# A hybrid decoder layer on one core: decay factors made a group sooner, a boundary weight rounded a step later, and the first 128 columns of keys and queries scaled straight from PSUM

## The chip, the cores and the metric

One Trainium2 chip, one core. The kernel is a hand-scheduled Tile program: one instruction stream for each engine, TensorE (PE), VectorE (DVE), ScalarE (ACT), GpSimd (POOL), and SyncE (SP), which issues most DMAs. The metric is device time in microseconds (us) of one launch. The times of the kernel before are 840.01, 841.22 and 841.30 us, with the median 841.22.

## The reference

The layer takes x of 512 tokens by 1024 features in float32 and adds three sub-layers to it, each with a norm ahead and behind:

```python
x = x + 0.5 * rms_norm(swiglu(rms_norm(x, ffn1_pre_g[l]), ffn1_w_gu[l], ffn1_w_down[l]), ffn1_post_g[l])
y = hybrid_mixer(rms_norm(x, mix_pre_g[l]), w_in[l], conv_w[l], conv_b[l], w_rg[l], ...)
x = x + rms_norm(y, mix_post_g[l])
x = x + 0.5 * rms_norm(swiglu(rms_norm(x, ffn2_pre_g[l]), ffn2_w_gu[l], ffn2_w_down[l]), ffn2_post_g[l])
```

`swiglu` has a hidden width of 2816. The mixer projects to four things: the input of a recurrence (512 channels), its gate (512), queries (8 heads of 64), and keys and values (2 heads of 64 each). The recurrence is a causal convolution of width 4, two block-diagonal gate products with a sigmoid, and a linear scan, whose decay is

```python
log_a = LRU_C * r * jax.nn.log_sigmoid(lam.astype(jnp.float32))
a = jnp.exp(log_a)
mult = jnp.sqrt(-jnp.expm1(2.0 * log_a))
```

`lam` has one value for each of the 512 channels, so `LRU_C * log_sigmoid(lam)` needs nothing but a parameter. Attention is banded: each block of 128 queries sees its own block of keys and the one before, and a sink. Block 0 has no block before it.

## The kernel before

Every float32 product is made of three matmuls on rounded parts: a weight is split into a high half (`whi`, cast by ACT) and a low half (`wlo`, what DVE finds by subtracting the high half from the raw weight), activations likewise. The class `Weights` (`W`) keeps three counters: raw weights loaded from HBM into five raw buffers, units rounded, units taken by a product. `W.fill(n)` rounds until `n` units beyond those taken are ready; a raw buffer that is used up is loaded anew at that point. `W.take(ahead)` fills ahead and hands out the next unit. So the place of a `fill` in the program sets where the cast and the subtraction of a weight stand in ACT's and DVE's streams. Each engine runs its stream strictly in the order in which it was written.

The first feed-forward part runs over five groups of hidden chunks (`GROUPS1`: 0-4, 4-8, 8-12, 12-16, 16-22), numbered 0 to 4. Groups 1 to 3 each run `octo`, a gate and an up product of four chunks at once by seven products instead of eight; its seven steps are numbered 0 to 6, each with two weight units and 24 matmuls (line L968), on the tiles `aa`, `da` and `ba`. From group 2 on, `seven_down` (L1362, tiles `yaa`, `yda`, `yba`, `yea`) multiplies the hidden values of the group before by the down weights, and `seven_forms_of` gives `octo` a dictionary `beside` of small steps to run after chosen steps: reading the hidden values back (`hxa`), sums of them (`s1a` to `s4a`) and their high (`hha`, `hhs`) and low (`hla`, `hls`) parts. `yea` is the product with the form `s4`.

`decay_factor` (L1290) computes `ka` = `LRU_C * log_sigmoid(lam)` and `nka` = -`ka` on a tile of 128 by 4: a few DVE operations, one `Exp` on ACT (`z`), and a series on DVE. ACT holds one table of functions at a time. A load of the table with `Exp` comes ahead of `z` (L1301), and a load of the table with `Silu` ahead of the next `Silu` (L995). The two results are first read in the mixer.

After group 4 comes the boundary to the mixer (`boundary`). The last three (`LATE`) of eight output chunks are taken aside as weights, and their products are made in two halves of 256 tokens: first half of chunks 5, 6 and 7, then the second halves. Each half is added to a partial sum (L697, `yp_a`), squared on ACT (L541, `sq_r`), and the squares are gathered (L710 and L714, `accb_r`). From them the statistics are made: a matmul with a mean vector (L555, `rms_r`), a square root on ACT (L561), a reciprocal (L563) and a diagonal tile `dg_r` (L565) on DVE, and a matmul that spreads it over the partitions (L569, `rms_r`). Both matmuls stand inside the second halves of chunks 6 and 7. Behind that the first products of the mixer use the four `xl` weights.

In the mixer, `in_parts` (L1548) takes a key or query product from its PSUM bank, scales it by the norm's factor `R` into a float32 tile, copies its first 128 columns into `home` (L1551), and splits the tile into high and low parts. `home` serves the plain float32 products of block 0 (`cur`, L1661), one call for the keys and four for the queries.

Of the kernel before, what the change touches and what calls it, by code (L numbers as in the profile page):

```python
# [15 lines left out]
P = 128  # L16
# [106 lines left out]
def tile_layer(ctx: ExitStack, tc: tile.TileContext, out: bass.AP, **ins: bass.AP):  # L123
    nc = tc.nc
    pe, dve, act, pool, sync = nc.tensor, nc.vector, nc.scalar, nc.gpsimd, nc.sync
# [37 lines left out]
    def wt(name, w=T, dt=F32):  # L163
        return tmp.tile([P, w], dt, tag="w", name=name, bufs=NW)


    W = Weights()
# [318 lines left out]
    def preload(func):  # L486
        act.activation(dummy, eps, func)
# [5 lines left out]
    def colrange(name):  # L493
        lo, n = col_of[name]
        return cols[:, lo:lo + n]
# [616 lines left out]
    def seven_down(hid, f, one, part, forms, ahead, beside={}, keep=False, hold=False):  # L1112

        free = [r_tile] + 3 * [acc_tile]
        for fn in beside.get(-1, ()):
            fn()
        A, B, Dd, E_ = ([bank(f"y{s}{hid.name}{f}{i}") for i in range(2)] for s in "abde")
        for n, (banks, form, blocks) in enumerate(((A, "a11", []), (Dd, "s3", [(1, 1)]), (B, "a12", [(0, 0)]), (A, "s2", [(1, 0)]),  # L1120
                                    (E_, "s4", [(0, 1)]), (Dd, "a22", [(1, 0)]), (A, "s1", [(1, 1), (0, 1)]))):
            if form == "s3":
                W.fill(AHEAD, True)
                hid.steps.pop(0)()
            one(banks, W.take(ahead if form == "a11" else AHEAD), forms[form], form in ("a11", "s3", "s4"))
            if form == "a11":
                for i in range(2):
                    act.copy(B[i], A[i])
            if hid.steps and form != "s3":
                hid.steps.pop(0)()  # L1130
            for i in range(2 if form in (("s3", "s2") if keep else ("a12", "s3", "s2", "s4") + (() if hold else ("a22", "s1"))) else 0):
                if keep:
                    o = part(*blocks[0], i)
                    dve.tensor_add(o, o, banks[i])
                    continue
                st = (wt if form == "s1" else free.pop() if free else t2k)("stage")
                act.copy(st, banks[i])  # L1137
                for half, dh in blocks:
                    o = part(half, dh, i)
                    pool.dma_start(o, st, accum_op=ALU.add)  # L1140
            for fn in beside.get(n, ()):
                fn()
        return {(0, 0): B, (1, 0): Dd, (0, 1): E_, (1, 1): A}
# [146 lines left out]
    def decay_factor():  # L1290

        lam = colrange("lru_lambda")

        def s4(name):
            return const.tile([P, KC], F32, name=name)

        nabs = s4("nabs")
        dve.tensor_scalar(nabs, lam, -1.0, None, op0=ALU.mult)
        dve.tensor_tensor(nabs, nabs, lam, op=ALU.min)
        z = s4("z")  # L1300
        act.activation(z, nabs, AF.Exp)  # L1301
        s = s4("s")
        dve.tensor_scalar(s, z, 2.0, None, op0=ALU.add)
        dve.reciprocal(s, s)
        dve.tensor_mul(s, s, z)
        s2 = s4("s2")
        dve.tensor_mul(s2, s, s)
        q = s4("q")
        dve.tensor_scalar(q, s2, 1.0 / 15, None, op0=ALU.mult)
        for n in (13, 11, 9, 7, 5, 3):  # L1310
            dve.scalar_tensor_tensor(q, q, 1.0 / n, s2, op0=ALU.add, op1=ALU.mult)
        dve.scalar_tensor_tensor(q, q, 1.0, s, op0=ALU.add, op1=ALU.mult)

        ka = s4("ka")
        dve.tensor_scalar(ka, lam, 0.0, LRU_C, op0=ALU.min, op1=ALU.mult)
        dve.scalar_tensor_tensor(ka, q, -2.0 * LRU_C, ka, op0=ALU.mult, op1=ALU.add)
        nka = s4("nka")
        dve.tensor_scalar(nka, ka, -1.0, None, op0=ALU.mult)
        return ka, nka
# [36 lines left out]
    hid = Hidden("a", n1)  # L1356
# [16 lines left out]
    def read_rows(dh):  # L1373
        if dh:
            t = wpool.tile([P, NB * T], F32, tag="raw", name="rows_a1", bufs=NRAW)
            row_sums[dh] = [t[:, tb * T:(tb + 1) * T] for tb in range(NB)]
        else:
            row_sums[dh] = [r_tile("rows_a00")] + [acc_tile(f"rows_a0{tb}") for tb in range(1, NB)]
        for tb in range(NB):
            sync.dma_start(row_sums[dh][tb], rows_hbm[tb, dh])  # L1380
# [3 lines left out]
    def turn_sums(dh):  # L1384
        z = wpool.tile([P, NB * T], F32, tag="raw", name="zy1", bufs=NRAW) if dh else wide("zy0")
        for tb in range(NB):
            row = row_sums[dh][tb]
            if dh or tb > 1:
                dve.tensor_add(row, row, held[tb // 2, dh][tb % 2])
            dve.transpose(z.rearrange("p (j b n) -> p b j n", n=32, b=NB)[:, tb], row.rearrange("p (j n) -> p j n", n=32))  # L1390
        moves[dh] = z

    def move_sums(dh):
        to = wide(f"yp_a{dh}")
        chunks = to.rearrange("p (c t) -> p c t", c=4)
        turned = moves[dh].rearrange("p (c q n) -> p c q n", c=4, q=4)
        for i in range(4):
            for q in range(4):
                (pool if q % 2 else sync).dma_start(chunks[32 * q:32 * (q + 1), :, i * P:(i + 1) * P], turned[32 * i:32 * (i + 1), :, q])  # L1399
        for c in range(4):  # L1400
            parts[4 * dh + c] = chunks[:, c]
# [26 lines left out]
    def give_back():  # L1428
        tiles, xT[:] = stream()
        for x, h in zip(tiles, xT_hbm):  # L1430
            pool.dma_start(x, h)
        return tiles

    parts = [None] * KD
    late, h_hbm, decay = [], {}, []
    for g, (f0, f1) in enumerate(GROUPS1):
        if g:
            beside = hid.seven_forms_of(before, h_hbm[before], dealt_halves=True) if g > 1 else {}
            if g == 2:
                beside[2] = [lambda: decay.append(decay_factor())]  # L1440
            h_hbm[f0] = hid.octo(f0, beside)
            if g > 1:
                held = seven_down(hid, before, by_dealt_tokens, lambda half, dh, i: rows_hbm[2 * half + i, dh], hid.forms, AHEAD - 1, hold=f1 == FC)
            if f1 == FC:
                held[0, 1] = held[1, 1]
                W.owed = [W.load, W.load, lambda: read_rows(1), lambda: None]
            before = f0
            if f1 < FC:
                continue
            xs = hid.last_chunks(f0, h_hbm[f0], {0: lambda: read_rows(0), 4: lambda: (turn_sums(0), move_sums(0))})  # L1450
            ka, nka = decay[0]
        else:
            hid.in_blocks = True
            first_down(hid.classic(f1, banks, {}))
            hid.in_blocks = False
            continue
        res = Residual("r1", lambda c: half_g[:, c:c + 1])
        turn_sums(1)
        for c in range(KD):
            if c == 0:  # L1460
                load_gates()
            if c == 1:
                move_sums(1)
                preload(AF.Sqrt)
            if c == 3:
                x_tiles[:] = give_back()
            if c >= KD - LATE:
                late.append((c, W.take(0)))
                W.fill(3)
                continue  # L1470
            if c == 0:

                two = [W.take(), W.take()]
                pair_banks = [bank(f"ya{g}{i}") for i in range(2)]
                for k, x in enumerate(xs):
                    for w, b in zip(two, pair_banks):
                        mm3(b, w, k, x, k == 0, k == len(xs) - 1)
            b = pair_banks[c] if c < 2 else product(W.take(), xs, name=f"ya{g}{c}")
            res.chunk(c, b, parts[c])
# [8 lines left out]
    def scaled(t, b):  # L1488
        dve.tensor_mul(t, b, R)
        return t  # L1490
# [53 lines left out]
    R = mx.R  # L1544
# [2 lines left out]

    def in_parts(b, first, name, low=dve):  # L1548

        x = scaled(wt(name), b)  # L1550
        dve.tensor_copy(first, x[:, :P])  # L1551
        if name == "qT3":
            spare.extend(fours("attn", F32R))
            xh, xl = spare.pop(), spare.pop()
        else:
            xh, xl = t2k(f"{name}h", F32R), t2k(f"{name}l", F32R)
        act.copy(xh, x)
        low.tensor_sub(xl, x, xh.bitcast(F32))
        return xh, xl
# [8 lines left out]
    for j in range(4):  # L1568
        b = in_product(f"pq{j}")
# [348 lines left out]
    hid = Hidden("b", n2)  # L1918
# [46 lines left out]
    h_hbm = {}  # L1965
# [27 lines left out]
    for g, (f0, f1) in enumerate(GROUPS2):  # L1993
        if g:
            h_hbm[f0] = hid.octo(f0, hid.seven_forms_of(before, h_hbm[before], (1, 2.5, 3.5, 4.5, 5.5, 6)), f1 == FC)
            kept = seven_down(hid, before, by_tokens, down, hid.forms, AHEAD - 1, *((last, True) if f1 == FC else ()))
            before = f0
# [15 lines left out]
        before = 2  # L2013
# [94 lines left out]
```

## Time and profile before

| what | value |
|---|---|
| median of the runs | 841.22 us (840.01 to 841.30) |
| the profiled execution | 840.68 us |
| its span, first to last instruction | 838.7 us |
| granted TensorE clock, mean | 0.999 |
| TensorE busy | 830.4 us (99%) |
| VectorE busy | 732.4 us (87%) |
| ScalarE busy | 519.2 us (62%) |
| GpSimd busy | 166.8 us (20%) |
| group 2: `octo` and `seven_down` | up to 175.04 us |
| boundary to the mixer | about 330 to 361 us |
| keys and queries of the mixer | about 371 to 408 us |

Rows of a timeline give start, duration, engine, line, operation, names of what is written and read, and in brackets how long the engine had stood idle and what ended that. Matmuls are pipelined: a row's duration is longer than the step to the next row, and a late matmul shows in the steps between starts. A matmul of 512 columns follows the one before by 0.23 us, one of 256 by 0.12. The chain of waits goes back from the last instruction to what released each step; merged rows give start, duration and the line. Rows of stretches give the busy time of each engine, with the number of instructions, the granted clock, the share of the DMA engines and GB/s.

### The profile page before, as it was taken

Reading aid. Unit: us, or ns where it says so; the run is one execution under the profiler, and the core shown is the slowest. Engines: PE = TensorE matmul, PEld = TensorE weight load, DVE = VectorE, ACT = ScalarE, POOL = GpSimd, SP = SyncE. Lnnn points to the kernel's source line nnn. Section 1 sums busy time; section 2 is a strip of 40 time slices with the busy share of each in tenths; the row PEclk is TensorE's granted clock in tenths of the full one; section 3 lists DMA queues with packets and bytes.
Section 4 is the critical chain, followed back from the end, with each engine's and each line's share of the span. In section 5 each row is a group of like instructions: output and inputs, shape, how many; then the busy total and the mean of one; then the engine's idle time right before and its main releaser. Section 6 shows DMA issues by size and latency. Waiting matters only on the chain.

```text
span 838.7 us, 11907 instructions
## 1 busy us (share of the span) xinstructions
PE 830.4 (99%) x4252; PEld 705.9 (84%) x4252; DVE 732.4 (87%) x1036; ACT 519.2 (62%) x813; POOL 166.8 (20%) x188
## 2 busy tenths in 40 slices
PE   9999999999999999999999999999999999999997
PEld 9988888788888898987788899888888888888885
DVE  4989698999989978889789589997999799898996
ACT  6646556586666654556797446545758667676562
POOL 2022000041320325414531052002004023032001
PEclk9999999999999999999999999999999999999999
DMA  7276407299595797522511131667339939769742
GB/s 252 102 274 227 150 11 263 100 254 301 118 259 188 181 283 228 188 82 88 158 51 51 51 114 39 127 173 252 104 116 243 314 84 255 239 153 260 299 142 101
DMA packets 121851, 144.22 MB, mean 172 GB/s; under 512 B 24184, under 2 KB 76736, under 8 KB 121280
## 3 DMA queue, kind: packets, MB, share of 16 engines
q1 hardware_dynamic: 107824, 112.91, 42.1%
q0 software_dynamic: 13824, 30.42, 16.5%
q8 instruction: 33, 0.54, 0.2%
q14 instruction: 26, 0.21, 0.1%
q10 hardware_dynamic: 144, 0.13, 0.0%
HBM read 100.45 MB, written 39.32 MB: 167 GB/s over the span
## 4 chain that ended last, share of the span: by engine, by line
PE 89%; DVE 6%; DMA 2%; ACT 1%; issue 1%; DVEq 0%; POOL 0%; ACTq 0%; POOLq 0%
PE ab L968 10%; PE aa L968 9%; PE db L968 5%; PE da L968 5%; PE bb L968 3%; PE ba L968 3%; PE ya L1362 3%; PE yaa L1362 2%; PE yda L1362 2%; PE a_first L1230 1%; PE yab L1949 1%; PE yab L1948 1%; PE yab L1947 1%; PE yea L1362 1%; PE mn L529 1%; PE an L529 1%
## 5 line engine op out<-in xcount | busy, mean ns | idle before, releaser
L1140 POOL DMA_DIRECT2D yr_a<-stage x36 | 31.6, 1014 | 177.9 <-ACT stage L1137 157.1
L1140 POOL DMA_DIRECT2D yp_b<-stage x42 | 36.5, 1062 | 147.1 <-ACT stage L1137 117.9
L1963 POOL DMA_DIRECT2D yp_b<-stage x8 | 4.4, 547 | 65.2 <-ACT stage L1962 64.8
L691 POOL TENSOR_TENSOR acca_r<-acca_r,sq_r 128x512 f32<-128x512 f32 x6 | 9.0, 1505 | 40.0 <-ACT sq_r L541 39.9
L529 PE MATMUL an<-xh_mx,whi_xl 128*128 128x256 f32 x64 | 15.9, 288 | 0.0
L530 PE MATMUL an<-xh_mx,wlo_xl 128*128 128x256 f32 x64 | 15.5, 283 | 0.0
L2066 POOL TENSOR_TENSOR last<-yp,grow 128x512 f32<-128x512 f32 x3 | 3.9, 1300 | 56.1 <-DVE yp L2056 56.1
L2063 ACT ACTIVATE ysq<-yp 128x512 f32<-128x512 f32 (+1 forms) x8 | 4.9, 607 | 16.2 <-DVE yp L2056 16.2
L511 PE MATMUL gt<-xh_mx,whi_gt 128*128 128x512 f32 x32 | 14.3, 446 | 0.0
L1399 POOL DMA_DIRECT2D yp_a<-zy x16 | 8.8, 555 | 25.4 <-DMA rows_a<-yr_a 17.2
L511 PE MATMUL pq<-xh_mx,whi_q 128*128 128x512 f32 x32 | 12.8, 400 | 0.0
L511 PE MATMUL pub<-xh_f,whi_bu 128*128 128x512 f32 x32 | 12.7, 395 | 0.0
L513 PE MATMUL gt<-xh_mx,wlo_gt 128*128 128x512 f32 x32 | 12.6, 394 | 0.0
L511 PE MATMUL pgb<-xh_f,whi_bg 128*128 128x512 f32 x32 | 12.6, 393 | 0.0
L512 PE MATMUL gt<-xl_mx,whi_gt 128*128 128x512 f32 x32 | 12.5, 392 | 0.0
L512 PE MATMUL pq<-xl_mx,whi_q 128*128 128x512 f32 x32 | 12.5, 391 | 0.0
L513 PE MATMUL pq<-xh_mx,wlo_q 128*128 128x512 f32 x32 | 12.5, 390 | 0.0
L513 PE MATMUL pgb<-xh_f,wlo_bg 128*128 128x512 f32 x32 | 12.5, 390 | 0.0
L513 PE MATMUL pub<-xh_f,wlo_bu 128*128 128x512 f32 x32 | 12.5, 389 | 0.0
L512 PE MATMUL pgb<-xl_f,whi_bg 128*128 128x512 f32 x32 | 12.5, 389 | 0.0
L512 PE MATMUL pub<-xl_f,whi_bu 128*128 128x512 f32 x32 | 12.5, 389 | 0.0
L1362 PE MATMUL ya<-whi_ad,hha 128*128 128x512 f32 x32 | 12.4, 389 | 0.0
(2018 smaller groups left out, 3415.9 us busy)
## 6 DMA issues: line engine op xcount, KB each, us to landing
yp_b<-stage POOLq DMA_DIRECT2D x50, 256.0 KB, 8.9
yr_a<-stage POOLq DMA_DIRECT2D x44, 256.0 KB, 9.7
h_a<-za SPq DMA_DIRECT2D x16, 256.0 KB
h_b<-zb SPq DMA_DIRECT2D x16, 256.0 KB
hxb<-h_b SPq DMA_DIRECT2D x16, 256.0 KB
hxa<-h_a SPq DMA_DIRECT2D x6, 512.0 KB
xn<-in_x SPq DMA_DIRECT2D x8, 256.0 KB
raw_ad<-in_ffn_w_down SPq DMA_DIRECT2D x2, 1024.0 KB
```

The source lines that it names most:

```text
L511: pe.matmul(ps, hi[:, k, :], xh, start=start, stop=False)
L512: pe.matmul(ps, hi[:, k, :], xl, start=False, stop=False)
L513: pe.matmul(ps, lo[:, k, :], xh, start=False, stop=stop)
L529: pe.matmul(ps[:, sl], hi[:, k, :], xh, start=k == 0 and not goes_on, stop=False, skip_group_check=True)
L530: pe.matmul(ps[:, sl], lo[:, k, :], xh, start=False, stop=False, skip_group_check=True)
L691: eng.tensor_add(acc, acc, square(part, ALL, f"{self.name}{c}"))
L968: pe.matmul(b[tb], x[:, blk], w[:, k, :], start=first and q + k + j == 0, stop=q + k == 2 and j == 2, skip_group_check=True)
L1140: pool.dma_start(o, st, accum_op=ALU.add)
L1230: pe.matmul(banks[j][:, HALF[0]], ws[j][part][:, k, :], n1.xs[k][xpart][:, HALF[0]], start=k == 0 and part == xpart, stop=stop and k == KD ...
L1362: pe.matmul(o, x[:, blk], a[:, k, :], start=start and j == 0, stop=stop and j == 2, skip_group_check=True)
L1399: (pool if q % 2 else sync).dma_start(chunks[32 * q:32 * (q + 1), :, i * P:(i + 1) * P], turned[32 * i:32 * (i + 1), :, q])
L1947: pe.matmul(banks[i], hh[:, js], hi[:, k, :], start=first and k == 0, stop=False, skip_group_check=True)
```

## The change

Three edits.

1. `decay_factor` is handed to `octo` as a side step in group 1 rather than in group 2, at the same step 2. In group 1 `beside` was empty.
2. In the loop over the output chunks, `W.fill` behind each chunk that is set aside asks for two units ahead rather than three. The units that are ready by then make this a change for one unit alone: the third `xl` weight is rounded inside `boundary` (its second `W.fill`) and not ahead of it.
3. In `in_parts` the first 128 columns are multiplied by `R` straight from the PSUM bank into `home`, ahead of the full multiplication, and are not copied from its result. This holds for all five calls.

```diff
-            beside = hid.seven_forms_of(before, h_hbm[before], dealt_halves=True) if g > 1 else {}
-            if g == 2:
-                beside[2] = [lambda: decay.append(decay_factor())]
+            beside = hid.seven_forms_of(before, h_hbm[before], dealt_halves=True) if g > 1 else {2: [lambda: decay.append(decay_factor())]}
             h_hbm[f0] = hid.octo(f0, beside)
...
             if c >= KD - LATE:
                 late.append((c, W.take(0)))
-                W.fill(3)
+                W.fill(2)
                 continue
...
     def in_parts(b, first, name, low=dve):
 
+        dve.tensor_mul(first, b[:, :P], R[:, :P])
         x = scaled(wt(name), b)
-        dve.tensor_copy(first, x[:, :P])
```

The order of the instructions on TensorE, GpSimd and SyncE is the same in both kernels. Two lines fewer stand in the file, so lines behind the first edit have numbers that are two lower in the changed kernel.

## The prediction

> **What bounds the kernel now.** I read the page first, then the chain of waits in order of time, then the timelines of VectorE (DVE), ScalarE (ACT) and TensorE (PE) around the edited places.
>
> ```profile
> PE 830.4 (99%) x4252; PEld 705.9 (84%) x4252; DVE 732.4 (87%) x1036; ACT 519.2 (62%) x813; POOL 166.8 (20%) x188
> PE 89%; DVE 6%; DMA 2%; ACT 1%; issue 1%; DVEq 0%; POOL 0%; ACTq 0%; POOLq 0%
> ...
> 300.00:320.00 20.00, 20.00 (x127) 18.11 (x126) 17.79 (x29) 8.34 (x15) 4.42 (x8) 1.00 0.82 266
> ```
>
> The last row is one of the stretches of 20 us (busy time of TensorE first, 20.00). TensorE is busy 99% of the span, and the change leaves its 4017 rows in the same order. So time can only come from the few places where a matmul starts late, and only new late starts can cost time. The chain leaves TensorE for long in three stretches: before 166.9, from 299 to 341, and from 449 to 463. Being on the chain isn't a late start; that is seen by equal work side by side. Groups 2 and 3 of the first feed-forward part have the same matmuls (L968, then L1362):
>
> ```profile
> 122.26 5.44 PE da L968 x24
> 175.04 5.44 PE aa L968 x24
> 180.48 5.44 PE da L968 x24
> 232.16 5.44 PE aa L968 x24
> ```
>
> From a group's first `da` to the first `aa` of the next group, group 2 takes 175.04 - 122.26 = 52.78 us and group 3 232.16 - 180.48 = 51.68. Group 2 loses **1.10 us**. The chain shows where, and DVE's and ACT's timelines show what made it late:
>
> ```profile
> 164.53 0.57 DVE s4a L880
> 166.24 0.61 DVE hls L851
> 166.89 2.58 PE yea L1362 x10
> ...
> 131.94 1.22 DVE L289 TENSOR_TENSOR wlo_at__1347<-raw_ax__1076,whi_at__1346 128x1024 fp32r<-128x1024 f32 x1
> 133.07 0.16 DVE L1298 TENSOR_SCALAR nabs<-cols 128x4 f32<-128x4 f32 x1
> 133.71 0.17 DVE L1303 TENSOR_SCALAR s<-z 128x4 f32<-128x4 f32 x1 [0.27 <-ACT z L1301]
> 136.45 1.22 DVE L289 TENSOR_TENSOR wlo_at__1366<-raw_ax__1095,whi_at__1365 128x1024 fp32r<-128x1024 f32 x1
> ...
> 129.30 1.28 ACT L1301 ACT_TABLE_LOAD   x1
> 133.47 0.21 ACT L1301 ACTIVATE z<-nabs 128x4 f32<-128x4 f32 x1 [2.88 <-DVE nabs L1299]
> 165.13 0.62 ACT L843 CAST hhs<-s4a 128x512 fp32r<-128x512 f32 x1 [6.85 <-DVE s4a L880]
> ```
>
> The decay chain holds DVE from 133.07 to 136.45, **3.38 us**, and DVE then works almost without a pause until `yea` has its operands.
>
> **Edit 1: the decay factors a group sooner.** 17 tiny DVE instructions, one ACTIVATE and its table load go from octo step 2 of group 2 to step 2 of group 1; another table load (L995, before the next Silu) goes along. The step issues no DMA. DVE before, in group 2 (`wlo_at` are low halves of weights, `nabs`, `s`, `q`, `ka` the chain):
>
> ```order
> L289 TENSOR_TENSOR wlo_at__1347<-raw_ax__1076,whi_at__1346 128x1024
> L1298 TENSOR_SCALAR nabs<-cols 128x4
> L1299 TENSOR_TENSOR nabs<-nabs,cols 128x4
> L1303 TENSOR_SCALAR s<-z 128x4
> L1304 RECIPROCAL s<-s 128x4
> L1305 TENSOR_TENSOR s<-s,z 128x4
> ```
>
> DVE now, in group 1, at the same step:
>
> ```order
> L289 TENSOR_TENSOR wlo_at__1054<-raw_ax__667,whi_at__1053 128x1024
> L1298 TENSOR_SCALAR nabs<-cols 128x4
> L1299 TENSOR_TENSOR nabs<-nabs,cols 128x4
> L1303 TENSOR_SCALAR s<-z 128x4
> L1304 RECIPROCAL s<-s 128x4
> ```
>
> The block has moved whole, between the two `wlo_at` of group 1. In group 2 DVE gets 3.38 us back and needs 1.10 of it; later waits for ACT or TensorE can eat some, but group 3, with the same work and no decay chain, loses nothing against it. So **-1.10 us**; bounds 0 (the chain was not the cause) and -1.10 (no more is lost there).
>
> What it costs in group 1:
>
> ```profile
> 91.23 1.23 DVE L289 TENSOR_TENSOR wlo_at__1073<-raw_ax__741,whi_at__1072 128x1024 fp32r<-128x1024 f32 x1 [1.22 <-ACT whi_at__1072 L285]
> 96.67 1.23 DVE L289 TENSOR_TENSOR wlo_au__1113<-raw_ay__885,whi_au__1112 128x1024 fp32r<-128x1024 f32 x1 [2.16 <-ACT whi_au__1112 L285]
> 90.15 1.05 ACT L285 CAST whi_at__1072<-raw_ax__741 128x1024 fp32r<-128x1024 f32 x1
> 103.06 0.39 PE L968 MATMUL aa<-whi_at__1072,t13h_a 128*128 128x512 f32 x1
> 92.48 0.88 SPq L175 DMA_DIRECT2D raw_ay__1148<-in_ffn_w_gu  x2
> 116.72 1.19 DVE L296 TENSOR_TENSOR raw_ax__1076<-raw_ay__1148,raw_ax__1076 128x1024 f32<-128x1024 f32 x1
> ```
>
> DVE idles here. `z` now stands behind the cast that ends at 91.20 and a table load of 1.28, so it is there at 92.7; the rest of the chain (133.71 to 136.45, 2.74 us) ends near 95.4 and `wlo_at__1073` near 96.7 instead of 92.46. Its first reader on TensorE starts at 103.06: 6.3 us of cover. If that is gone, each further microsecond is a late matmul. The 4.2 us of delay are taken up by waits such as the 2.16 above. What is queued behind: the load of `raw_ay__1148`, issued when `wlo_at__1073` ends, goes from 92.48 to about 96.8, with its first reader at 116.72; on ACT the second table load (1.28) stands ahead of the next Silu, whose result only DVE reads, two products of 5.44 us later. Cost 0.
>
> **Edit 2: one weight rounded a step later.** The third `xl` weight's cast (ACT) and subtraction (DVE) move behind the second half-chunk of the boundary. DVE before (`yp_a` adds a chunk's partial sum, `accb_r` gathers squares for the norm):
>
> ```order
> L215 TENSOR_TENSOR wlo_xl_0_3248<-raw_xl__3189,whi_xl_0_3247 128x1024
> L697 TENSOR_TENSOR yp_a_3135<-ay_3268,yp_a_3135 128x256
> L710 TENSOR_TENSOR accb_r_3070<-acca_r_3069,sq_r_3288 128x256
> L697 TENSOR_TENSOR yp_a_3135<-ay_3291,yp_a_3135 128x256
> L714 TENSOR_TENSOR accb_r_3070<-accb_r_3070,sq_r_3311 128x256
> ```
>
> DVE now:
>
> ```order
> L697 TENSOR_TENSOR yp_a_3135<-ay_3264,yp_a_3135 128x256
> L710 TENSOR_TENSOR accb_r_3070<-acca_r_3069,sq_r_3284 128x256
> L697 TENSOR_TENSOR yp_a_3135<-ay_3287,yp_a_3135 128x256
> L714 TENSOR_TENSOR accb_r_3070<-accb_r_3070,sq_r_3307 128x256
> L215 TENSOR_TENSOR wlo_xl_0_3311<-raw_xl__3189,whi_xl_0_3310 128x1024
> ```
>
> The subtraction no longer stands ahead of two chunks that are ready. The trace there, and the same two handovers where nothing waits (496.61 to 497.10, and 350.21 to 350.57):
>
> ```profile
> 333.32 1.05 ACT L210 CAST whi_xl<-raw_xl__3189 128x1024 fp32r<-128x1024 f32 x1 [2.03 <-DMA raw_xl__3189<-in_w_in]
> 334.40 1.23 DVE L215 TENSOR_TENSOR wlo_xl<-raw_xl__3189,whi_xl 128x1024 fp32r<-128x1024 f32 x1 [2.20 <-ACT whi_xl L210]
> 339.06 0.42 DVE L714 TENSOR_TENSOR accb_r<-accb_r,sq_r 128x256 f32<-128x256 f32 x1 [0.48 <-ACT sq_r L541]
> 340.90 0.42 DVE L565 TENSOR_TENSOR dg_r<-ident,rs_r 128x256 f32<-128x256 f32 x1
> 339.33 0.28 PE L513 MATMUL ay<-hha,wlo_ad 128*128 128x256 f32 x1
> 340.01 0.37 PE L511 MATMUL ay<-hha,whi_ad 128*128 128x256 f32 x1
> 341.05 0.28 PE L513 MATMUL ay<-hha,wlo_ad 128*128 128x256 f32 x1
> 341.79 0.47 PE L511 MATMUL ay<-hha,whi_ad 128*128 128x256 f32 x1
> 496.61 0.28 PE L513 MATMUL my<-ylh,wlo_wo 128*128 128x256 f32 x1
> 497.10 0.36 PE L511 MATMUL my<-attn,whi_wo 128*128 128x256 f32 x1
> 350.21 0.28 PE L530 MATMUL an<-xh_mx,wlo_xl 128*128 128x256 f32 x1
> 350.57 0.47 PE L529 MATMUL an<-xh_mx,whi_xl 128*128 128x256 f32 x1
> ```
>
> Cast and subtraction sat until the load of `raw_xl__3189` came, with the first chunk's add behind them. The statistics matmuls cost 0.68 us of TensorE instead of 0.49 (they wait for `accb_r`, which ends at 339.48), the spread 0.74 instead of 0.36 (it waits for `dg_r`): 0.19 + 0.38 = 0.57 us lost. Now the last `accb_r` of the first half waits for the cast (it follows the second chunk's square: half-chunks are 18 matmuls of 0.12 us, so that chunk's product ends near 334.3, its add and square near 335.2; cast to 336.3), the subtraction (to 337.5), then add, square and sum, 0.42 each with handovers: about 338.9, 0.6 before TensorE wants it. The 0.19 goes. Of the 0.38 some stays: from the statistics the path over ACT, reciprocal and `dg_r` is serial, and starts only 0.2 earlier; the reciprocal also no longer queues behind an `accb_r`. I take 0.16 of it, so **-0.35 us**, between 0 (another wait takes over) and -0.57.
>
> **Edit 3: `home` straight from PSUM.** Five copies of 128 columns become five multiplications ahead of the full one.
>
> ```profile
> L1551 DVE COPY home<-qT x4: 226/711/1140, 394.9 to 407.1; 128x128 f32<-128x128 f32 x4
> L1551 DVE COPY home<-kT x1: 866/866/866, 382.8 to 382.8; 128x128 f32<-128x128 f32 x1
> 397.06 2.14 POOL L1536 TENSOR_TENSOR xcl<-xc,xch 128x512 fp32r<-128x512 f32 x1 [0.93 <-ACT xch L1535]
> 399.66 0.49 PE L1517 MATMUL rg<-xch,gates 64*128 64x512 f32 x1
> PE rms_lru L555 <- DVE acc_lru L1863: 0.3, 1, 0.3
> ```
>
> No row shows a 128-column multiplication from PSUM; the 256-column adds from PSUM take 0.42, a copy that waits for nothing 0.23. I take 0.3, nearer the copy in size. DVE gains about 0.87 + 4 x 0.71 - 5 x 0.3 = 2.2 us, but TensorE doesn't wait for `home`, so that is worth 0. On the other side `kT` and each `qT` come 0.3 later, with the casts behind them on ACT; the nearest reader is the gate product at 399.66, whose `xcl` is done at 399.20, 0.46 ahead. **0**, between -0.3 (the wait of the last row, at 462, shrinks) and +0.7 (the multiplications wait as the copies did, up to 1.14: 1.14 - 0.46).
>
> The copies took 0.61 to 1.14 whenever GpSimd was working, and 0.23 alone. The Trainium skill (SBUF — State Buffer, "Who interferes with whom") says that a copy in a two-port mode and a GpSimd instruction lock each other out, while a DVE instruction with at most one SBUF input does not contend. By that rule the new multiplications, one operand in PSUM, never wait, and the edit's upper end would be 0 instead of +0.7; the trace's copies agree with its first half, and no row of before tests the second.
>
> **Sum.** The profiled execution took 840.68 us, of which the span is 838.7. 840.68 - 1.10 - 0.35 + 0 = 839.23. The median of the runs is 841.22, 0.54 above that execution; from it the same sum gives 839.77. I forecast the middle, **839.5**.
>
> **Rivals.**
> - *The first gain is half given back* (a transfer is late instead). From 299 to 327 the chain runs over DMA: if those transfers don't move forward with TensorE, the sum that is needed at 339.4 is needed 1.1 earlier but is only 0.6 ahead; 0.5 returns: 840.68 - 0.95 = 839.7, or 840.3 from the median. For it: 2% of the chain is DMA. Against: TensorE is busy throughout there (the row for 300 to 320). Chance 0.15.
> - *The multiplications wait like the copies.* +0.7 at the gate products: 839.9 to 840.5. Chance 0.07.
> - *More is gained*: the rest of the 0.57 goes, and the 0.3 at 462 too: 840.68 - 1.97 = 838.7. Against: ACT is the partner in both chains. Chance 0.13.
> - *Slower*: the moved weight now stands ahead of the third chunk's add, and its load decides. In the trace the load landed just before 333.32. Later than about 335.8 it delays cast, subtraction and `accb_r` one for one; the gain of 1.45 is gone at 337.3, and the kernel is 0.2% (1.7 us) slower at 339. If TensorE arrives earlier and the load, fed by a queue that is full, does not, it goes that way. Against: that needs 5.7 us. 842.9, chance 0.10.
> - *The change doesn't do what it says*, because the decay chain isn't what makes group 2 late: only -0.35, 840.3 to 840.9. Chance 0.05.
>
> **How the numbers follow.** The likeliest case has 0.50. 0.2% of 841.22, 1.68 us, is about what a measurement of this kernel can tell from no change, and the forecast, 1.72 below, lies at that bound: of its 0.50 I put 0.34 on faster and 0.16 on same. With 0.13 from the larger gain: faster 0.47. Same: 0.16 + 0.15 + 0.07 + 0.05 = 0.43; slower 0.10. The range runs from 838.4 (840.68 - 1.10 - 0.57 - 0.6) to 841.2, which takes in all but the slower case.
>
> **What the changed profile would show.** Group 2 from `da` to the next group's `aa` in 51.7 us; ACT's wait for `s4a` shorter; in group 1 the second `wlo_at` near 96.7 and no late matmul at 103; the statistics and spread in about 0.49 and 0.6; `home` rows near 0.3 whatever GpSimd does. I am wrong if a late start appears in group 1, at the boundary or at the gate products, or if group 2 still takes 52.8.

## The result and the profile after

The changed kernel takes 839.33 us (median of 18 runs, 838.66 to 839.97), the kernel before 840.68 us (18 runs beside them on the same chip, 839.52 to 842.34). The ratio is 0.9984, with a 95% interval of 0.9978 to 0.9990: 1.35 us less, between 0.8 and 1.9. The forecast was 839.5. The gain of 0.16% lies just inside the bound of 0.2%, beyond which a change was to count as faster. The profiled execution has a span of 837.6 us against 838.7.

The page first: the busy times, and the chain that ended last.

```profile
PE 829.3 (99%) x4252; PEld 705.7 (84%) x4252; DVE 730.5 (87%) x1036; ACT 520.0 (62%) x813; POOL 166.4 (20%) x188
PE 96%; DVE 2%; DMA 1%; SPq 0%; issue 0%; ACT 0%; DVEq 0%; ACTq 0%
```

VectorE's part of the chain has gone from 6% to 2%, though it works only 1.9 us less than before: what has gone is its place on the path. The chain now runs through groups 2 and 3 on TensorE alone. The rows are the first `da` of group 2, `yea` in it, the first `aa` of group 3, the first `da` of group 3, and the first `aa` behind that group (a merged row of this chain starts about 0.17 us later than its first matmul in the timeline):

```profile
122.59 5.44 PE da L968 x24
166.11 2.72 PE yea L1362 x12
174.27 5.44 PE aa L968 x24
179.71 5.44 PE da L968 x24
231.39 4.76 PE aa L968 x21
```

Group 2 takes 174.27 - 122.59 = 51.68 us, as group 3 does, and 1.10 less than before. On VectorE and ScalarE, the sum that `yea` reads, and its cast, come well ahead of it:

```profile
160.96 0.65 DVE L880 SCALAR_TENSOR_TENSOR s4a<-s2a,hxa 128x512 f32<-128x512 f32 x1
161.64 0.62 ACT L843 CAST hhs<-s4a 128x512 fp32r<-128x512 f32 x1 [3.03 <-DVE s4a L880]
```

In before `s4a` starts at 164.53; ScalarE's wait for it fell from 6.85 to 3.03 us. In group 1, where the decay chain stands now, VectorE and ScalarE show:

```profile
93.07 0.17 DVE L1303 TENSOR_SCALAR s<-z 128x4 f32<-128x4 f32 x1 [2.42 <-ACT z L1301]
95.82 1.22 DVE L289 TENSOR_TENSOR wlo_at__1073<-raw_ax__741,whi_at__1072 128x1024 fp32r<-128x1024 f32 x1
101.78 1.23 DVE L289 TENSOR_TENSOR wlo_av__1170<-raw_ay__885,whi_av__1169 128x1024 fp32r<-128x1024 f32 x1 [1.33 <-ACT whi_av__1169 L285]
91.54 1.28 ACT L1301 ACT_TABLE_LOAD   x1
92.83 0.21 ACT L1301 ACTIVATE z<-nabs 128x4 f32<-128x4 f32 x1
```

VectorE waits 2.42 us for `z`, the second `wlo_at` ends at 97.04, and by 101.78 VectorE waits for ScalarE again: the delay is made up, and no matmul of group 1 starts late. At the boundary, TensorE, ScalarE and VectorE:

```profile
338.58 0.28 PE L513 MATMUL ay<-hha,wlo_ad 128*128 128x256 f32 x1
339.06 0.36 PE L511 MATMUL ay<-hha,whi_ad 128*128 128x256 f32 x1
340.10 0.28 PE L513 MATMUL ay<-hha,wlo_ad 128*128 128x256 f32 x1
340.62 0.47 PE L511 MATMUL ay<-hha,whi_ad 128*128 128x256 f32 x1
334.34 1.03 ACT L210 CAST whi_xl<-raw_xl__3189 128x1024 fp32r<-128x1024 f32 x1
335.41 1.23 DVE L215 TENSOR_TENSOR wlo_xl<-raw_xl__3189,whi_xl 128x1024 fp32r<-128x1024 f32 x1 [0.52 <-ACT whi_xl L210]
337.45 0.43 DVE L714 TENSOR_TENSOR accb_r<-accb_r,sq_r 128x256 f32<-128x256 f32 x1 [0.49 <-ACT sq_r L541]
```

The statistics cost TensorE 0.49 us (0.68 before), the spread 0.53 (0.74 before); starts in rows are rounded, so their differences can be 0.01 off. The cast starts as soon as ScalarE is free, where before it waited 2.03 us for the weight's load. The last `accb_r` of the first half ends at 337.88, 0.8 us before it is read. The new multiplications into `home`, with GpSimd's row that runs beside the last of them:

```profile
397.06 0.28 DVE L1548 TENSOR_TENSOR home<-pq,R_mx 128x128 f32<-128x128 f32 x1
405.19 0.29 DVE L1548 TENSOR_TENSOR home<-pq,R_mx 128x128 f32<-128x128 f32 x1
404.12 2.12 POOL L1522 TENSOR_TENSOR xc<-ig,xc 128x512 f32<-128x512 f32 x1 [0.72 <-DMA ig<-other]
```

All five take 0.28 to 0.29 us, also beside GpSimd, where the copies took up to 1.14.

These gains add up to 1.10 + 0.20 + 0.21 = 1.51 us, while the span fell by 1.15. In this execution the first matmuls started later: group 1's first `da` starts at 84.35, and at 84.02 in the execution of before. Among the profiles below whose tiles lie where they lay, this start is between 83.85 and 84.95 us, a scatter of 1.1 us that no edit explains.

### The profile page after: what moved, and what is told of

It reads as the page before. It is cut to its first block, busy times and chain, and to the rows that moved or that the text cites. A ratio compares the mean times of both kernels' runs of the same rounds, so it can differ in the third digit from the quotient of the medians.

```text
span 837.6 us, 11902 instructions
## 1 busy us (share of the span) xinstructions
PE 829.3 (99%) x4252; PEld 705.7 (84%) x4252; DVE 730.5 (87%) x1036; ACT 520.0 (62%) x813; POOL 166.4 (20%) x188
## 3 DMA queue, kind: packets, MB, share of 16 engines
q0 software_dynamic: 13824, 30.42, 16.5%
## 4 chain that ended last, share of the span: by engine, by line
PE 96%; DVE 2%; DMA 1%; SPq 0%; issue 0%; ACT 0%; DVEq 0%; ACTq 0%
PE ab L968 10%; PE aa L968 10%; PE db L968 5%; PE da L968 5%; PE yaa L1362 3%; PE bb L968 3%; PE ba L968 3%; PE ya L1362 3%; PE yda L1362 2%; PE aa L898 1%; PE a_first L1230 1%; PE yab L1945 1%; PE yab L1946 1%; PE yab L1947 1%; PE yea L1362 1%; PE yba L1362 1%
## 5 line engine op out<-in xcount | busy, mean ns | idle before, releaser
L511 PE MATMUL gt<-xh_mx,whi_gt 128*128 128x512 f32 x32 | 14.3, 447 | 0.0
L511 PE MATMUL pq<-xh_mx,whi_q 128*128 128x512 f32 x32 | 12.8, 400 | 0.0
L511 PE MATMUL pub<-xh_f,whi_bu 128*128 128x512 f32 x32 | 12.6, 395 | 0.0
L513 PE MATMUL gt<-xh_mx,wlo_gt 128*128 128x512 f32 x32 | 12.6, 394 | 0.0
L511 PE MATMUL pgb<-xh_f,whi_bg 128*128 128x512 f32 x32 | 12.6, 393 | 0.0
L513 PE MATMUL pq<-xh_mx,wlo_q 128*128 128x512 f32 x32 | 12.5, 390 | 0.0
L513 PE MATMUL pgb<-xh_f,wlo_bg 128*128 128x512 f32 x32 | 12.5, 390 | 0.0
L513 PE MATMUL pub<-xh_f,wlo_bu 128*128 128x512 f32 x32 | 12.5, 390 | 0.0
```

What stands on the lines that cost most here:

```text
L511: pe.matmul(ps, hi[:, k, :], xh, start=start, stop=False)
L513: pe.matmul(ps, lo[:, k, :], xh, start=False, stop=stop)
```

## The experiments

All ratios are to the kernel before, run on the same chip beside it, with 95% intervals. For each, a difference in us is worked out from the two medians. Beside the times, TensorE's starts were read in each trace, in us: when the first `da` of group 1 starts; from there to the first `da` of group 2 ("group 1"); from that to the first `aa` of group 3 ("group 2"); from there to the last L513 ahead of the statistics ("to the boundary"); the two handovers at the boundary, from the last L513 ahead of the statistics or spread matmuls to the next L511; from that L511 to the matmul behind the last spread of the mixer's norms ("mixer"); and from there to the last matmul:

| kernel | first `da` of group 1 | group 1 | group 2 | to the boundary | statistics, spread | mixer | behind it |
|---|---|---|---|---|---|---|---|
| before | 84.02 | 38.08 | 52.78 | 164.45 | 0.68, 0.74 | 166.57 | 323.78 |
| after | 84.35 | 38.08 | 51.68 | 164.47 | 0.49, 0.53 | 166.57 | 323.80 |
| edit 1 alone | 83.85 | 38.08 | 51.68 | 164.41 | 0.61, 0.75 | 166.60 | 323.77 |
| edit 2 alone | 84.79 | 38.08 | 52.86 | 164.47 | 0.49, 0.53 | 166.59 | 323.78 |
| edit 3 alone | 84.95 | 38.08 | 52.80 | 164.69 | 0.52, 0.75 | 166.93 | 323.79 |
| after, table loads back | 84.31 | 38.08 | 51.68 | 164.41 | 0.49, 0.53 | 166.95 | 323.80 |
| after, a `wo` weight later | 84.82 | 38.08 | 51.68 | 164.46 | 0.49, 0.53 | 166.77 | 323.80 |
| after, 24 more, in place | 84.22 | 38.08 | 51.68 | 164.41 | 0.49, 0.53 | 166.67 | 323.79 |
| after, 52 more, in place | 84.09 | 43.29 | 51.68 | 164.41 | 0.49, 0.53 | 167.02 | 323.79 |
| before, 24 more, in place | 84.50 | 38.08 | 57.67 | 164.46 | 1.03, 0.75 | 167.03 | 323.78 |
| after, tiles 32 bytes on | 85.49 | 38.08 | 51.68 | 167.56 | 0.49, 0.52 | 166.90 | 324.96 |

Where an edit leaves group 1, group 2 or the part behind the mixer alone, they repeat to within 0.1 us; the stretch to the boundary does so too but for edit 3 alone (0.2 to 0.3 more, ahead of the place of that edit) and the last row. That is finer than the medians, so it is by this table that the edits are told apart. The start and the mixer scatter: the mixer takes about 166.6 or 167.0 us, the second where three transposes of the attention (at 442 us) each start 0.15 late. Both values occur with edit 3 and without it.

**The three edits alone.** Each kernel is before with one hunk of the diff.

> The kernel before with edit 1 alone (decay factors in group 1). Theory: the chain on VectorE is what made group 2 late, so -1.1 us against before; group 2 from its first da to the next aa 51.7 us instead of 52.8, the boundary's two handovers as before (0.68 and 0.74 us). Rival (the chain isn't the cause): 0, and group 2 still takes 52.8.

Measured: 839.99 us against 841.07, ratio 0.9988 (0.9979 to 0.9997), 1.08 us less. Group 2 takes 51.68, and the spread still costs 0.75, as the theory said.

> The kernel before with edit 2 alone (third xl weight a step later). Theory: the two handovers at the boundary shrink from 0.68 and 0.74 to about 0.48 and 0.52, -0.4 us against before; group 2 keeps its 52.8. Rival (the gain came only because TensorE arrived at another moment after edit 1): 0, handovers as before. Rival (the weight's load is late without edit 1): more than 0.

Measured: 841.09 against 841.07, ratio 0.9999 (0.9990 to 1.0008). No gain is seen in the time, though one of 0.4 is within the interval. In the trace the handovers do shrink, without edit 1. TensorE's rows at the boundary of this kernel:

```profile
340.20 0.28 PE L513 MATMUL ay<-hha,wlo_ad 128*128 128x256 f32 x1
340.68 0.36 PE L511 MATMUL ay<-hha,whi_ad 128*128 128x256 f32 x1
341.72 0.28 PE L513 MATMUL ay<-hha,wlo_ad 128*128 128x256 f32 x1
342.25 0.47 PE L511 MATMUL ay<-hha,whi_ad 128*128 128x256 f32 x1
```

They are 0.49 and 0.53, as after. So by the trace the edit shortens the spread by itself, and the rival with a late load falls; the time alone would not tell. The other rival, TensorE's moment of arrival, falls for the spread (0.75 in edit 3 alone, where TensorE arrives 0.3 us later still), but not for the statistics. How much it brings is less sure: the spread costs 0.74 to 0.75 in the kernels without the edit that have no other work added and 0.53 with it, but the statistics cost 0.68, 0.61 or 0.52 without it, depending on the execution, and 0.49 with it. So 0.2 us is steady, and 0.03 to 0.19 comes on top. The traces show on what that depends. Without the edit the cast of this weight waits for its load: it starts 6.17, 6.08 and 6.01 us ahead of the last L513 in edit 3 alone, edit 1 alone and before, and the statistics cost 0.52, 0.61 and 0.68; below, in before with 24 more in place, it starts 5.66 ahead and they cost 1.03. Each tenth of a microsecond by which the load lands later is lost. With the edit the cast starts 4.24 us ahead and has no load to wait for, and the cost is 0.49 in every such profile. The edit takes this dependence away.

> The kernel before with edit 3 alone (home scaled straight from PSUM). Theory: five instructions of 0.28 us instead of copies of 0.23 to 1.14, some 2 us off VectorE, and no matmul waits for them: 0 us (within 0.2). Rivals: -0.3 if VectorE is earlier at the wait at 462; +0.3 or more if the later full scaling delays the gate products.

Measured: 841.63 against 841.07, ratio 1.0006 (0.9997 to 1.0015). The five multiplications take 0.28 us, and none of the gate products starts late. The 0.56 by which the median is higher lies within an interval that holds zero. In the profiled execution, whose span is 1.35 longer, the start makes 0.93, the stretch to the boundary 0.24 and the transposes of the mixer 0.36; the first two stand ahead of the edit. No gain and no loss of the edit is seen; a loss of some tenths that comes by way of the start is not excluded by the runs.

**Which part of the chain made group 2 late.** After, with this in addition:

```diff
+            if g == 2:
+                beside[2] = [lambda: preload(AF.Exp)]
```

> The kernel after with ScalarE's two table loads (1.28 us each) and one 128x1 ACTIVATE put back at the old place in group 2, while VectorE's chain stays in group 1. Theory (VectorE's hold of 3.38 us was the cause): as after, -1.35 us against before, and group 2 takes 51.7. Rival (ScalarE's table loads were the cause): group 2 takes 52.8 again, about -0.3 against before.

Measured: 839.96 against 841.07, ratio 0.9986 (0.9977 to 0.9995), 1.11 us less. ScalarE has a load again there (its timeline), and TensorE doesn't notice. Of ScalarE's rows:

```profile
129.58 1.28 ACT L487 ACT_TABLE_LOAD   x1
```

and of its chain:

```profile
122.55 5.44 PE da L968 x24
174.23 5.44 PE aa L968 x24
```

174.23 - 122.55 = 51.68: the table loads were not the cause. What this run doesn't put back is ScalarE's wait of 2.88 us for VectorE's `nabs`. That VectorE's own 3.38 us count rests on the run below that adds work to VectorE alone in group 2.

**How much cover each place has.** Into `decay_factor`, ahead of `ka`, go 25 or 53 VectorE instructions of 128 by 4, each waiting for the one before:

```diff
+        hold = s4("hold")
+        dve.tensor_scalar(hold, s2, 1.0 / 15, None, op0=ALU.mult)
+        for n in range(24):
+            dve.scalar_tensor_tensor(hold, hold, 1.0 / 13, s2, op0=ALU.add, op1=ALU.mult)
```

> The kernel after with 25 more VectorE instructions of 128x4 (serial, about 0.2 us each by the six that take 94.08 to 95.27) inside the chain in group 1: 5.0 us more hold. Theory (in group 1 there are 6.3 us of cover): as after, -1.35 us against before, no late matmul. Rival (no cover, VectorE's time there counts): +5.0 against after, +3.6 against before.

> The same with 53 more such instructions: 10.5 us more hold. Theory: the 6.3 us of cover are used up and each further microsecond is a late matmul: 4.2 us against after, +2.9 against before, and the late start stands where the second wlo_at of group 1 is first read. Rival (other waits take up the delay): as after. Rival (no cover): +10.5 against after.

> The kernel before with the same 25 instructions in the chain at its old place, in group 2. Theory: there the slack is already used up (3.38 us of hold cost 1.10), so the 5.0 us are lost one for one: +5.0 us against before, group 2 in 57.8. Rival (slack of the size of group 1): 0. Half of it, if VectorE catches up between forms: about +2.5.

Measured: 846.03 with 24 in group 1 (ratio 1.0061, 1.0049 to 1.0074), 851.19 with 52 (1.0124, 1.0109 to 1.0138), and 854.36 with 24 in group 2 of before (1.0161, 1.0147 to 1.0174), against 840.63. That is 5.4, 10.6 and 13.7 us more: by their times the theory fails in all three. The first two lie nearer the rival that no cover is there (3.6 and, from its 10.5 against after, 9.2), and 1.8 and 1.4 above it. The traces don't fit that rival. With 24 instructions in group 1 no matmul of groups 1 and 2 is late (with 52 one is, by 3.6 us). With 24, the late starts are before 23 us, ahead of the added instructions, at 315 us, and at 766 to 809, in the second feed-forward part, which has nothing to do with the decay chain. The transfer engines spent more time on the same bytes.

What the three share beside the instructions is the tile `hold`. In the built kernels, whose addresses no profile shows, tiles stand in order at multiples of 32 bytes in each partition, so everything behind `hold` begins 32 bytes further on: the first large tile at byte 18464 and not at 18432. The next four runs take the two apart.

**The same instructions without a tile.** They write into `nabs`, which nobody reads any more:

```diff
+        dve.tensor_scalar(nabs, s2, 1.0 / 15, None, op0=ALU.mult)
+        for n in range(24):
+            dve.scalar_tensor_tensor(nabs, nabs, 1.0 / 13, s2, op0=ALU.add, op1=ALU.mult)
```

> The kernel after with the same 25 extra instructions in the chain in group 1, written into nabs, which is dead by then, so that no tile is added and no address moves. Theory (group 1 has 6.3 us of cover; what was lost with the hold tile came from the addresses of the tiles behind it, 32 bytes further on): as after, about -1.3 us against before. Rival (25 more VectorE instructions cost time wherever they stand, by their time or their code): about +5.4 again.

Measured: 839.73 against 841.20, ratio 0.9984 (0.9976 to 0.9993), 1.5 us less, as after. VectorE and TensorE of this kernel in group 1:

```profile
95.42 4.70 DVE L1315 SCALAR_TENSOR_TENSOR nabs<-nabs,s 128x4 f32<-128x4 f32 x24
100.50 1.22 DVE L289 TENSOR_TENSOR wlo_at__1073<-raw_ax__741,whi_at__1072 128x1024 fp32r<-128x1024 f32 x1
103.48 0.39 PE L968 MATMUL aa<-whi_at__1072,t13l_a 128*128 128x512 f32 x1
103.71 0.39 PE L968 MATMUL aa<-wlo_at__1073,t13h_a 128*128 128x512 f32 x1
```

The second `wlo_at` ends 4.7 us later than in after, at 101.72, and its first reader still starts on time, 0.23 after the matmul ahead. So 4.7 more microseconds on VectorE cost nothing here, and 2 us of cover are left.

> The same with 53 extra instructions. Theory: the second wlo_at of group 1 ends about 107.4, 4 us after TensorE wants it; the run with the hold tile showed 3.6 us of late start there and then nine matmuls at a granted clock of about 0.59 (0.43 us apart instead of 0.23), so 3.6 + 1.8 = +5.4 us against after, +4.1 against before. Rival (each microsecond beyond the cover costs just one): +3.6 against after, +2.3 against before. Rival (the tile's addresses don't matter): +10.5 against before, as with the hold tile.

Measured: 845.24 against 841.20, ratio 1.0048 (1.0036 to 1.0061): 4.0 more than before, 5.5 more than with 24. TensorE's rows:

```profile
103.36 0.39 PE L968 MATMUL aa<-whi_at__1072,t13l_a 128*128 128x512 f32 x1
107.18 0.80 PE L968 MATMUL aa<-wlo_at__1073,t13h_a 128*128 128x512 f32 x1 [3.44 <-DVE wlo_at__1073 L289]
109.05 0.63 PE L968 MATMUL aa<-whi_at__1072,t13h_a 128*128 128x512 f32 x1
109.48 0.63 PE L968 MATMUL aa<-whi_at__1072,t13l_a 128*128 128x512 f32 x1
```

Stretches of the span, with their length, the busy time of TensorE, of its weight loads, of VectorE, ScalarE and GpSimd, then the granted clock, the transfer engines' share and GB/s:

```profile
103.00:107.00 4.00, 0.74 (x4) 0.28 (x2) 3.52 (x17) 1.82 (x3) 0.00 (x0) 0.99 0.00 0
107.00:110.40 3.40, 3.22 (x8) 2.57 (x9) 3.40 (x4) 0.59 (x1) 0.00 (x0) 0.51 0.57 160
110.40:120.00 9.60, 9.60 (x44) 7.92 (x43) 9.60 (x13) 2.66 (x4) 0.00 (x0) 1.00 0.48 163
```

The matmul that reads the late weight starts 3.82 after the one ahead, 3.6 too late. Then the granted clock is 0.51 for 3.4 us: matmuls follow each other by 0.43 and not 0.23. Group 1 takes 43.29 - 38.08 = 5.21 us longer, 3.6 of it the wait and 1.6 the slow matmuls behind it. So here a microsecond beyond the cover cost more than one. The Trainium skill (TensorE: Matmul & The Clock Gate, "What's actually happening") says that TensorE falls back to half of its clock after an idle window of about 3.4 us, and that it takes as long a busy window to be let up again. This trace agrees, with 3.44 us of waiting and 3.4 us at 0.51.

> The kernel before with the 25 extra instructions at the old place in group 2, written into nabs. Theory (there the cover is used up, VectorE's time counts one for one): +5.0 us against before, perhaps 1 to 2 more where the stalls are long enough for TensorE's granted clock to drop; group 2 from its first da to the next aa in 57.8 or more. Rival (cover as in group 1): 0.

Measured: 846.81 against 841.20, ratio 1.0068 (1.0056 to 1.0081), 5.6 more. Group 2 takes 57.67, 4.89 more for 25 instructions that hold VectorE 4.9 us: one for one, at three places (TensorE's rows, with what ended its wait):

```profile
143.03 0.50 PE L968 MATMUL aa<-wlo_at__1366,t13h_a 128*128 128x512 f32 x1 [0.80 <-DVE wlo_at__1366 L289]
152.45 0.50 PE L968 MATMUL aa<-whi_av__1475,b2h_a 128*128 128x512 f32 x1 [1.41 <-ACT u4a L973]
171.13 0.49 PE L1365 MATMUL yea<-whi_adt__1617,hhs 128*128 128x512 f32 x1 [1.99 <-ACT hhs L843]
```

The third, of 1.99 us, is ahead of `yea`, where before started late too. The granted clock stayed at 1.00 behind it. Of the waits in these runs, those of 3.42 (52 more with the tile) and 3.44 us halved the clock and this one didn't; none lies between. Another 0.35 us is lost at the boundary's statistics (1.03 and not 0.68). The same 25 instructions cost nothing in group 1 and all their time in group 2; that is the whole of edit 1.

**The addresses alone.** After, with no instruction more:

```diff
-    dummy = const.tile([P, 1], F32, name="dummy")
+    dummy = const.tile([P, 16], F32, name="dummy")[:, :1]
```

> The kernel after with no instruction added, only the dummy tile of 4 bytes per partition made 64 bytes wide, so that every tile allocated behind it begins 32 bytes further on (18464 instead of 18432 for the first large one: a multiple of 32, no longer of 64). Theory (these addresses slow the transfers into SBUF): about +5 us against before, with late matmuls where the loads are the partner (from 8 to 23, at 315, from 766 on), and a larger share of the transfer engines for the same bytes (GpSimd's queue 17.0% instead of 16.5%). Rival (addresses are nothing, the extra instructions were it): as after, -1.35.

Measured: 845.25 against 841.20, ratio 1.0051 (1.0037 to 1.0065), 4.05 us more than before and, against after's 1.35 less, 5.4 us for 32 bytes. Set against the trace of after, it starts 1.1 us later, loses 3.1 between group 3 and the boundary, 0.3 in the mixer and 1.2 behind it. Of its page, the transfer queues with packets, MB and the share of 16 engines' span:

```profile
q1 hardware_dynamic: 107824, 112.91, 42.7%
q0 software_dynamic: 13824, 30.42, 17.1%
```

TensorE's waits in this kernel, each with its sum, count and longest:

```profile
PE ya L511 <- ACT hha L905: 1.1, 1, 1.1
PE ydb L1947 <- DVE hla L851: 0.8, 1, 0.8
PE ya L512 <- DVE hla L837: 0.7, 1, 0.7
PE a_first L529 <- ACT xh_a L585: 0.6, 1, 0.6
```

Of these after has none.

The page of after has, for the same packets and bytes:

```profile
q1 hardware_dynamic: 107824, 112.91, 42.0%
q0 software_dynamic: 13824, 30.42, 16.5%
```

GpSimd's queue (q0) took 17.1% of 843.5 us and not 16.5% of 837.6: 4.4% more time for each byte, and q1 2.4% more. It has 16.4 or 16.5% in all ten kernels here whose large tiles begin at 18432, and 17.0 or 17.1% in the four where they begin at 18464. The engines are not slower: VectorE is busy for 730.6 us here and 730.5 in after, GpSimd 166.0 and 166.4. The chain of this kernel shows what that does, where the first feed-forward part sends its sums out to memory and reads them back as `rows_a`:

```profile
299.26 9.14 DMA rows_a<-yr_a
308.49 0.70 DVE rows_a L1389
```

In before such a transfer is on the chain too, with 7.70 us, and no matmul there waits; in after it isn't on the chain, which stays on TensorE from 285 to 323 us. Here the waits for `hla` and `hha` in the list, at 315 and 318 us, come behind it. In the second feed-forward part the chain to the wait for `hla` of `ydb` at 810 starts from a transfer too (`yp<-yp_b`, 7.40 us from 782.6). The Trainium skill (DMA: Bandwidth & Descriptors, "How a descriptor splits into AXI transactions") says that a transaction must start at a multiple of 256 bytes, so that a descriptor that starts elsewhere also fetches the bytes from the multiple below, which cost bus beats and aren't used. 18432 is such a multiple and 18464 is not, so the trace agrees in direction. That this is the mechanism is not shown, nor whether 256 is the bound, or 64.

**One more wait.** What still stands on the path is the wait of 0.30 for `acc_lru` at 461. In this kernel, after with the low half of a `wo` weight moved behind the sums of squares:

```diff
     scale_rows(NB - 1)
-    deferred.run()
...
         add_square(ci)
+    deferred.run()
     preload(AF.Sqrt)
```

> The kernel after with one more edit: the second deferred wo weight's low half (1.22 us on VectorE at 450.27, ahead of the scans) is written behind the sums of squares of the recurrent branch. Theory: what TensorE waits for at 460.9 (461 ns late) is acc_lru at the end of VectorE's queue, so that wait goes, -0.45 us against after, -1.8 against before. Rival: the weight is now late for its first matmul at 462.84 instead, 0 or slower than after.

Measured: 839.51 against 840.63, ratio 0.9987 (0.9979 to 0.9996), 1.1 us less than before, so not better than after. VectorE's rows show why:

```profile
454.11 0.69 DVE L1487 TENSOR_TENSOR G<-gt,R_mx 128x512 f32<-128x512 f32 x1 [0.60 <-PE gt L513]
459.98 2.28 DVE L1860 TENSOR_TENSOR acc_lru<-acc_lru,sq_l 128x512 f32<-128x512 f32 x3
```

With 1.22 us of work out of the way VectorE now waits 0.60 us for the last gate product, so the sums come only 0.2 us earlier against TensorE, and the late start goes from 0.46 to 0.23. The weight that was moved isn't late: it is done at 463.39, and its first matmul starts at 463.54. The mixer of this kernel took 166.77, 0.2 less than in the other executions with late transposes. The expectation of 0.45 was twice too much.

## Why the prediction was right

- *The number, and some luck.* The terms add up to 1.45 us and 1.35 was measured. That the time of 839.33 lies so near to 839.5 is partly luck: the forecast stands halfway between a sum from 840.68 and one from 841.22, and the kernel before took 840.68 in the longer series. Of the chances, faster (0.47) was put ahead of same (0.43); the measured 0.16% is on the side of same. The "4017 rows" of TensorE are 4252 on the page of either kernel.
- *The view.* TensorE's busy share doesn't find the gain; two groups with equal work do. 52.78 against 51.68 was the whole size of edit 1, and the time followed: 1.10 in the trace, 1.08 in the runs of edit 1 alone.
- *Edit 1, cause.* VectorE's hold, not the table loads that moved along. The run with the loads put back excludes these, and the one with 24 more on VectorE in group 2 shows that its time counts there. The rival by which half is given back at a transfer fell: from group 3 to the boundary after takes 164.47 us and before 164.45.
- *Edit 1, cost at the new place.* The second `wlo_at` was forecast for 96.7 and ended at 97.04, in an execution whose group 1 starts 0.33 later. The cover is real: 4.7 us more on VectorE were free, with 2.0 left, so it was 6.7, and 10.2 us more came 3.6 too late. It is 0.4 more than the 6.3 forecast, because the row taken there reads the high half; the low half's first reader is two matmuls later (0.45). "Each further microsecond is a late matmul" was too mild: behind a wait of 3.44 us, 1.6 us more were lost to the granted clock.
- *Edit 2.* The term of 0.35 measured 0.41 between the two traces (0.20 and 0.21). The half that was chosen by judgement, 0.16 of the spread's 0.38, is the one that repeats (0.2); the statistics' 0.19, which was taken as sure, is 0.03 to 0.19 by the execution, as the weight's load lands. The weight was ready 2.06 us ahead of the statistics matmuls (336.64 against 338.70); the forecast had 2.04 (337.5 against 339.54). The load was there in time, and the rival with a late load fell for that reason.
- *Edit 3.* 0 for the time within what the runs can tell, 0.28 us for one multiplication (estimate 0.3), and VectorE's busy time 1.9 us less with all three edits, 1.3 with edit 3 alone (forecast 2.2). The rule of the Trainium skill that was weighed there (SBUF — State Buffer, "Who interferes with whom"), that an instruction with one operand in SBUF doesn't contend with GpSimd, agrees with the rows at 397.06 and 405.19. With it goes the rival of +0.7.
- *What wasn't foreseen* is the start, whose 0.33 us in these two profiles is as large as edit 2. Of this 0.22 is a wait for the first load of x; with edit 3 alone such waits make 0.70 of 0.93. It is why the two profiled spans differ by 1.15 and not by the 1.51 of the terms. The runs of the three edits alone add up to about -0.5 and not to the -1.35 of the whole; each has an interval of some 0.8 us to either side, so this says nothing against the terms, and that the start makes the difference is not shown.

## What to carry to other kernels

Small serial work that nobody waits for belongs where its engine idles: the same chain cost 1.1 us beside `seven_down` and nothing one group earlier, and the size can be read ahead of time from two stretches with equal work. Check a place's cover by adding work there, and add it without a new tile: a tile of 16 bytes that pushes all others by 32 bytes cost four times what the three edits bring together. Where a change is smaller than the scatter of the runs, compare stretch by stretch in the traces.

## What the hardware showed that was not expected

- 32 bytes of offset for all tiles behind the first few made the transfers of the two large queues 2.4 and 4.4% longer and the kernel 5.4 us slower, with no instruction changed. With other work added in group 1 the same offset cost 6.3 us (846.03 - 839.73) and 6.0 us (851.19 - 845.24), in group 2 of before 7.6 us (854.36 - 846.81). In these three pairs the kernel before took 840.63 beside the first and 841.20 beside the second; taken against it, each difference is 0.6 us larger.
- A wait of 3.44 us on TensorE halved the granted clock for the next 3.4 us (0.51); one of 1.99 us didn't.
- A load that landed some tenths of a microsecond later, relative to TensorE, cost the same tenths at the boundary (0.52 to 1.03 us for the statistics); one weight rounded later made it 0.49 always.
- Serial VectorE instructions of 128 by 4 cost 0.196 us each: 24 in 4.70 us, 52 in 10.2.
